# An output projection that prepares its operands two tiles ahead, with rows and values turned in squares by VectorE

## The chip, the cores and the metric

The kernel runs on one core of a Trainium2 chip. The metric is the time of one execution on the device, in microseconds (us). Before the change the median of three runs is 2102.44 us (2100.62 to 2109.52).

The engines are TensorE (PE; its weight loads are PEld), VectorE (DVE), ScalarE (ACT), GpSimd (POOL) and SyncE (SP). SP does no arithmetic here: it issues transfers, and so can ScalarE. A queue issues its transfers in order, and one that has to wait holds up those behind it.

## The reference

One inference step of a two-layer encoder, in fp32, on a prompt of 2048 tokens and on a second sequence of 32 ("sampled") tokens that carries its own state; width 1024. The kernel puts both in one list of 2080 rows, 17 tiles of 128 (the last has 32).

```
# layer 1: gated delta rule
proj = x @ w_in                      # 1024 -> 4112; short causal conv, silu, l2norm
o, s = gated_delta_rule(q, k, v, g, beta, s0)
o = rmsnorm(o) * norm_w * silu(z)    # "g" in the kernel
h = layer_norm(ALPHA * x + o @ w_out, ln_g, ln_b)
# shared keys and values of layer 2
k, v = rope(h @ w_k), h @ w_v        # 256 columns each
# layer 2: sliding-window attention with sinks
q, z = rope(h @ w_q) / 8, h @ w_z    # 1024 columns each
y = layer_norm(ALPHA * h + (attention(q, k, v) * silu(z)) @ w_out2, ln_g2, ln_b2)
```

The outputs are y for both sequences, and the new states and caches. Every large product is made of three products of fp32r operands: a value is split into a high part (a cast) and a low part (value minus high part), and high x high, high x low and low x high are summed.

## The kernel before, in words

Stages follow each other with overlaps. `P1` projects x and convolves. `Delta` runs the delta rule in chunks of 128 rows; its steps are one pipeline whose order is a string in the class (`ORDER`), with an offset for each step that says which chunk it works on. `O1` is the first layer's output projection, with its layer norm. `P2` projects h to the second layer's keys, values, queries and gates. `Attention` does the rest.

**O1.** A tile of 128 rows needs `g` (the gated outputs, columns on partitions, 128x8x128), split into `g_hi` (ScalarE) and `g_lo` (VectorE), and `r` (the rows of x). For each half of the 1024 columns (c = 0, 1) `OutNorm.tile` makes 24 matmuls into one bank of PSUM (`po`, two banks), and then VectorE adds the bank to ALPHA * r and takes statistics. After the second half VectorE makes the inverse deviation in a chain of small steps (Newton's method on one column), and normalises with two fused steps for each half (L1203, L1205), both of which read two tensors from SBUF. The rows are stored to `h`. `O1.turned` then turns them, since P2 needs columns on partitions: eight transposes on TensorE in two groups of four (L1232), into a bank each, copied by ScalarE or VectorE into `hT`, stored in pieces of 512 bytes. These two groups are issued inside the next tile's product, after its seventh and eighth step.

`O1.tiles` is a generator: it yields after every six matmuls with an estimate of their time, eight times a tile. While Delta runs, a `Filler` pulls from it: `give(0.45)` after each TensorE step of the last two rounds, and more in `first_end`. What is left runs in `second.rest()` at the end of Delta. The tile ahead is fetched at a tile's start, split after its fourth step; g has one buffer, r two, g_hi and g_lo two each.

In `rest()` TensorE and VectorE have a hand-written order (the order of the program); ScalarE, GpSimd and the queues are ordered by a planner, which may move work ahead of the place where the program has it.

`more(i)` puts other work between tiles: before tile 8 the split of P2's first operand block (`load0`), before tiles 11 to 14 a quarter each of the sums of operands that P2 needs (`presum`: four loads, four GpSimd subtractions, four stores), after tile 15 the first two products of P2 and after tile 16 the next four. `P2.go(n)` pulls n half products from `P2.stream`, which also issues weights 12 products ahead, casts them 3 ahead and makes low parts 2 ahead.

**P2.** Two pairs of 416-column blocks are multiplied with Strassen's scheme in seven products instead of eight (`group`), one block is multiplied singly. All five engines have a hand-written order here. `delay(f, n)` runs f n products later. `operand` casts an operand's four quarters on ScalarE and makes low parts on VectorE. `out_weights` is pulled one step with each product that has an operand: it loads, splits and stores the second layer's output weights, one of 16 parts every eight steps, with the cast on ScalarE two products after the load's issue. `P2.turn` turns a values product (128 columns x 416 rows): four transposes on TensorE into the bank `tp` (L1714), two copies on ScalarE, two stores from ScalarE's queue in pieces of 512 bytes. Banks of PSUM in P2: X and Z two each, Y one, tp one, two for single products.

`first_end` (in Delta) finishes the sampled chunk, which was computed first: it loads its outputs and gates, turns and gates them, stores g, and gives time to O1, all after the last chunk's step `OSC`.

## Time and profile before

| | |
|---|---|
| median of three runs | 2102.44 us (2100.62 to 2109.52) |
| profiled execution | 2110.58 us, of which the span of the profile is 2108.8 |
| TensorE, VectorE, ScalarE, GpSimd busy | 97%, 70%, 47%, 43% of the span |
| O1 alone, in its hand-written order | about 1132 to 1333 us of the span |
| P2 | about 1333 to 1740 |
| attention | 1740 to the end |

Times inside the execution are microseconds from the span's start. A row of a timeline has start, duration, engine, line, operation, and out<-in; in brackets is how long the engine stood idle before it, and what released it. A row of a group has a count, total busy time, mean in ns, and the idle time before the group's instructions. TensorE's matmuls overlap: one of 512 columns is shown with 390 ns, and the next begins 227 ns after it. The granted clock is the share of TensorE's full clock that the chip allowed in a stretch.

### The profile page before, as it was taken

What the parts mean: (1) busy time and instruction counts of PE and PEld (TensorE: products, weight loads), DVE (VectorE), ACT (ScalarE), POOL (GpSimd) and SP (SyncE); (2) the same over time, 40 slices, a digit from 0 to 9 for tenths busy, and PEclk for the clock granted to TensorE, in tenths of its full rate; (3) what the DMA queues carried; (4) which work ended last, traced back from release to release, by engine and by line L of the source; (5) the groups of instructions that cost most, each with busy time, mean ns of one, the idle gap of its engine ahead of it and who ended that gap; (6) DMA issues with size and microseconds to landing.
All of it is one profiled execution on the core that took longest, in us unless ns stands there. A gap on an engine that the chain in (4) does not pass through costs nothing.

```text
span 2108.8 us, 37301 instructions
## 1 busy us (share of the span) xinstructions
PE 2048.6 (97%) x13694; PEld 1875.4 (89%) x13694; DVE 1468.9 (70%) x2587; ACT 989.0 (47%) x2465; POOL 911.0 (43%) x1248
## 2 busy tenths in 40 slices
PE   7999999999999999999999999999999999999998
PEld 5999999999999999999887887889989997777775
DVE  4476666675647678888887887768877755566565
ACT  4354444446532267777762211534644445455552
POOL 0322223212222177778752112157436515566666
PEclk9999999999999999999999999999999999999999
DMA  5132333236665545455766666778776659533421
GB/s 206 33 90 88 97 110 111 82 102 226 193 185 179 182 137 179 159 169 182 271 209 227 212 213 219 254 229 296 243 240 222 226 171 317 127 101 107 114 72 66
DMA packets 292763, 360.85 MB, mean 171 GB/s; under 512 B 74260, under 2 KB 217460, under 8 KB 292564
## 3 DMA queue, kind: packets, MB, share of 16 engines
q1 hardware_dynamic: 278576, 334.29, 49.9%
q10 hardware_dynamic: 14004, 24.17, 3.6%
q8 instruction: 108, 1.77, 0.3%
q14 instruction: 75, 0.61, 0.1%
HBM read 235.54 MB, written 134.06 MB: 175 GB/s over the span
## 4 chain that ended last, share of the span: by engine, by line
PE 83%; DMA 7%; DVE 3%; POOL 3%; issue 2%; ACT 1%; SPq 0%; ACTq 0%; DVEq 0%; POOLq 0%
PE ps L79 12%; PE ps L81 11%; PE ps L80 11%; PE ot L1126 3%; PE ot L1127 3%; PE ot L1128 3%; PE S L1992 2%; PE po L1126 2%; PE ot L2025 2%; PE po L1128 2%; PE po L1127 2%; PE tr L2007 2%; PE X L1653 2%; PE X L1651 2%; PE X L1652 2%
## 5 line engine op out<-in xcount | busy, mean ns | idle before, releaser
L79 PE MATMUL ps<-act_hi,w_hi 128*128 128x416 f32 x1280 | 454.9, 355 | 0.0
L81 PE MATMUL ps<-act_hi,w_lo 128*128 128x416 f32 x1280 | 450.2, 352 | 0.0
L80 PE MATMUL ps<-act_lo,w_hi 128*128 128x416 f32 x1280 | 447.9, 350 | 0.0
L79 PEld LDWEIGHTS ps<-act_hi,w_hi 128*128 128x128 f32 x1280 | 240.3, 188 | 3.8 <-issue 0.4
L80 PEld LDWEIGHTS ps<-act_lo,w_hi 128*128 128x128 f32 x1280 | 240.6, 188 | 3.0
L81 PEld LDWEIGHTS ps<-act_hi,w_lo 128*128 128x128 f32 x1280 | 240.1, 188 | 3.3
L209 DVE SCALAR_TENSOR_TENSOR y<-R,convw,y 128x2083 f32<-128x2083 f32 x72 | 182.5, 2536 | 60.9 <-ACT y L206 44.9
L56 POOL TENSOR_TENSOR w_lo<-w_raw,w_hi 128x1024 fp32r<-128x1024 f32 x25 | 71.4, 2858 | 330.9 <-ACT w_hi L55 303.6
L729 POOL TENSOR_TENSOR tm<-L,Tt 128x60 f32<-128x60 f32 (+19 forms) x365 | 132.5, 363 | 84.8 <-issue 39.9
L1826 POOL TENSOR_TENSOR P<-e,sm 128x384 f32<-128x384 f32 (+2 forms) x128 | 102.3, 820 | 118.0 <-DVE sm L1816 111.6
L731 POOL TENSOR_TENSOR Tt<-Tt,tm 128x60 f32<-128x60 f32 (+19 forms) x365 | 139.8, 383 | 28.6
L1812 ACT ACTIVATE e<-S,nm 128x193 f32<-128x193 f32 (+2 forms) x260 | 104.6, 415 | 97.3 <-DVE nm L1807 56.5
L1330 DVE TENSOR_TENSOR w_lo<-w_raw,w_hi 128x512 fp32r<-128x512 f32 x132 | 136.7, 1053 | 18.5 <-ACT w_hi L1342 12.7
L1126 PE MATMUL po<-wo_hi,g_hi 128*128 128x512 f32 x256 | 104.9, 410 | 8.1 <-DVE r L1134 7.9
L305 ACT COPY R<-ps 128x416 f32<-128x416 f32 (+1 forms) x144 | 60.4, 442 | 109.3 <-PE ps L81 95.8
L1482 ACT ACTIVATE o<-X 128x416 f32<-128x416 f32 x80 | 41.4, 518 | 134.7 <-PE X L1653 134.6
L1126 PE MATMUL ot<-wo,g_hi 128*128 128x512 f32 x256 | 103.6, 405 | 0.0
L1128 PE MATMUL po<-wo_hi,g_lo 128*128 128x512 f32 x256 | 101.2, 396 | 0.5 <-DVE g_lo L1169 0.5
L1127 PE MATMUL po<-wo_lo,g_hi 128*128 128x512 f32 x256 | 101.1, 395 | 0.0
L1127 PE MATMUL ot<-wo,g_hi 128*128 128x512 f32 x256 | 100.8, 394 | 0.0
L1128 PE MATMUL ot<-wo,g_lo 128*128 128x512 f32 x256 | 100.8, 394 | 0.0
L1342 ACT CAST w_hi<-w_raw 128x512 fp32r<-128x512 f32 x129 | 76.8, 616 | 21.5 <-PE ps L1652 6.7
(362 smaller groups left out, 5119.4 us busy)
## 6 DMA issues: line engine op xcount, KB each, us to landing
w_raw<-in_b_w SPq DMA_DIRECT2D x60, 512.0 KB
w_raw<-in_w_in SPq DMA_DIRECT2D x40, 512.0 KB
act_raw<-s_hT SPq DMA_DIRECT2D x64, 208.0 KB
s_rows<-o SPq DMA_DIRECT2D x50, 208.0 KB
k<-s_k SPq DMA_DIRECT2D x17, 512.0 KB
E<-s_E SPq DMA_DIRECT2D x17, 512.0 KB
s_bq<-s_rows SPq DMA_DIRECT2D x40, 208.0 KB
s_bz<-o SPq DMA_DIRECT2D x40, 208.0 KB
```

The costliest lines, as they stand in the source:

```text
L79: nc.tensor.matmul(ps, hi[:, k, :], xh[:, k, :], start=(k == 0), stop=False)
L80: nc.tensor.matmul(ps, hi[:, k, :], xl[:, k, :], start=False, stop=False)
L81: nc.tensor.matmul(ps, lo[:, k, :], xh[:, k, :], start=False, stop=(k == KC - 1))
L209: nc.vector.scalar_tensor_tensor(out=y[:], in0=R[:, j:j + W], scalar=self.convw[:, i, j:j + 1], in1=y[:], op0=ALU.mult, op1=ALU.add)
L729: P.tensor_tensor(out=tm[:n, i0 - k:, :w], in0=L[:n, i0:, j:j + 1].to_broadcast(sh), in1=Tt[:n, j:j + 1, :w].to_broadcast(sh), op=ALU.mult)
L731: P.tensor_tensor(out=Tt[:n, i0:, :w], in0=Tt[:n, i0:, :w], in1=tm[:n, i0 - k:, :w], op=ALU.subtract)
L1126: nc.tensor.matmul(ps[:n], ghi[:, k, :n], hi, start=a, stop=False)
L1127: nc.tensor.matmul(ps[:n], ghi[:, k, :n], lo, start=False, stop=False)
L1128: nc.tensor.matmul(ps[:n], glo[:, k, :n], hi, start=False, stop=z)
L1330: P.tensor_tensor(out=lo, in0=raw, in1=hi, op=ALU.subtract)
L1812: self.nc.scalar.activation(x.e[:, h, u, :x.n], x.S[:, h, u, :], AF.Exp, bias=x.nm[:, h, u:u + 1], scale=1.0, accum_out=x.sm[:, h, u:u + 1])
L1826: self.nc.gpsimd.tensor_tensor(out=x.P[:, u, :nj * 128].rearrange("r (j h k) -> r j h k", h=2, k=64), in0=x.e[:, :, u, :n].rearrange("r h ...
```

## The change

1. **O1's pipeline.** `split` becomes `cast` (ScalarE) and `low` (VectorE). Two tiles are prepared before the loop; in tile i, after the second step, the low part of tile i+1's g (cast at the end of tile i-1) is made and g of tile i+2 is fetched. The layer norm of a tile moves into the tile after it: `scaled` after its first step, a ScalarE activation for mean and deviation after its second, `affine` (two VectorE steps over 1024 columns and the store to `h`) after its fourth, before the addition of its own first half, `turned` after its fifth, the load of the next tile's rows after its seventh. All transfers of O1 are issued by SP. The second half's bank comes from P2's two single-product banks once they exist (`spare`), so four banks are used.
2. **Rows turned by VectorE.** `turned` is one VectorE transpose that turns each 32x32 square of the 128x1024 rows in place of its square; four stores, one for each 32 partitions, put the squares in place in `hT`, in pieces of 128 bytes (32 rows of one column). The tile `hT` has two buffers; during Delta it lies in the buffers of its k.
3. **Values turned by VectorE.** `P2.turn` likewise: one transpose of 128x416, four stores on SP in pieces of 128 bytes, one to four products later. The bank tp goes, and Y has two.
4. **Other work spread.** `more(i)` is taken one step after each step of a tile: P2's first twelve steps (weights) in tiles 3 to 5, `load0` two quarters at a time in tiles 6 to 9, the sums from tile 11 on with steps between the loads, each subtraction and the stores, P2's first operand loads and two products before tile 16, four products after it.
5. **Order.** `rest()` has a hand-written order on TensorE, VectorE, ScalarE and SP. Delta's sampled end is loaded at the last round's start and done after step R, not after OSC; one more call of the generator is made before. `out_weights` begins eight steps later.

The order of O1's loop, and the new functions, from the diff:

```diff
@@ OutNorm @@
+    def bank(self, c):
+        if c and self.spare:
+            return self.spare()
+        return self.pp.tile([128, 512], F32, tag="po", name="po")
+
+    def cast(self, g, n):
         ghi = self.two.tile([128, KC, 128], F32R, tag="g_hi", name="g_hi")
+        self.nc.scalar.copy(ghi[:, :, :n], g[:, :, :n])
+        return ghi
+
+    def low(self, g, ghi, n):
         glo = self.two.tile([128, KC, 128], F32R, tag="g_lo", name="g_lo")
-        nc.scalar.copy(ghi[:, :, :n], g[:, :, :n])
-        nc.vector.tensor_tensor(out=low_part(ghi, glo, n), in0=g[:, :, :n], in1=ghi[:, :, :n], op=ALU.subtract)
+        self.nc.vector.tensor_tensor(out=low_part(ghi, glo, n), in0=g[:, :, :n], in1=ghi[:, :, :n], op=ALU.subtract)
         return ghi, glo
...
+    def scaled(self, r, n, st):
...
-                V.scalar_tensor_tensor(out=r[:n, cs], in0=r[:n, cs], scalar=mv[:n, 0:1], in1=tabs[0][:n, cs],
-                                       op0=ALU.subtract, op1=ALU.mult)
-                V.scalar_tensor_tensor(out=r[:n, cs], in0=r[:n, cs], scalar=rs[:n, 0:1], in1=tabs[1][:n, cs],
-                                       op0=ALU.mult, op1=ALU.add)
-        yield r
+        nb = self.two.tile([128, 1], F32, tag="nb", name="nb")
+        V.tensor_scalar(out=nb[:n], in0=mv[:n, 0:1], scalar1=rs[:n, 0:1], scalar2=-1.0, op0=ALU.mult, op1=ALU.mult)
+        return lambda: nc.scalar.activation(r[:n], r[:n], AF.Identity, bias=nb[:n, 0:1], scale=rs[:n, 0:1])
+
+    def affine(self, r, n, st):
+        V, tabs = self.nc.vector, self.tabs
+        V.tensor_tensor(out=r[:n], in0=r[:n], in1=tabs[0][:n], op=ALU.mult)
+        V.tensor_tensor(out=r[:n], in0=r[:n], in1=tabs[1][:n], op=ALU.add)
@@ O1 @@
     def turned(self, h, c0, row, n):
...
+        hT = self.room().rearrange("p a b -> p (a b)")
+        self.nc.vector.transpose(hT[:n], h[:n])
+        rows = self.T["hT"].rearrange("h (c j) t -> j (h c) t", j=32)
+        for a in range(0, n, 32):
+            self.nc.sync.dma_start(rows[:, :, c0 + a:c0 + a + 32],
+                                   hT[a:a + 32].rearrange("j (c i) -> j c i", i=32))
 
     def tiles(self, tiles, ready, more):
...
+            beside = itertools.chain(beside, more(i))
+            if i + 1 == len(tiles):
+                yield from (out for out in beside if out)
+            for j, out in enumerate(on.tile(parts.pop(0), r, t[2])):
+                yield out
+                next(beside, None)
+                if j == 0 and last:
+                    normalise = on.scaled(*last)
+                elif j == 1:
+                    if last:
+                        normalise()
+                    for c in coming:
+                        parts.append(on.low(g, high, c[2]))
+                    coming = tiles[i + 2:i + 3]
+                    for c in coming:
+                        while not ready(c):
+                            yield 1.0
+                        g = self.fetch(*c)
+                elif j == 3 and last:
+                    self.affine(last, *tiles[i - 1])
+                elif j == 4 and last:
+                    self.turned(last[0], *tiles[i - 1])
+                if j == 6 and i + 1 < len(tiles):
+                    following = self.rows(*tiles[i + 1])
+            for c in coming:
+                high = on.cast(g, c[2])
+            last, r = (r, t[2], on.stats), following
@@ P2 @@
-        self.py = new_pool(self.tc, left, "p2_py", 1, PSUM, side="left")
+        self.py = new_pool(self.tc, left, "p2_py", 2, PSUM, side="left")
...
     def out_weights(self):
...
+        for _ in range(8):
+            yield
...
     def turn(self, c, half, b):
...
+        nc, t = self.nc, self.out()
+        nc.vector.transpose(t[:], c[:])
...
+        def store(a):
+            s = slice(32 * a, 32 * a + 32)
+            nc.sync.dma_start(rows[a], t[s].rearrange("i (b j) -> i b j", j=32))
+
+        for a in range(4):
+            self.delay(lambda a=a: store(a), 1 + a)
@@ program @@
     def more(i):
-        if i == 0:
-            p2[0].load0()
-        elif i >= 3:
-            drain(p2[0].presum(0, p2[0].raw_act, 0, (i - 3,)))
-        else:
-            yield from p2[0].go(4 * i)
+        if 3 <= i < 6:
+            for _ in range(4):
+                next(p2[0].main)
+                yield
+        elif 6 <= i < 10:
+            yield from p2[0].load0(2 * i - 12)
+        elif 11 <= i < 15:
+            yield from p2[0].presum(0, p2[0].raw_act, 2, (i - 11,), 3)
+        elif i == 16:
+            p2[0].first_loads()
+            yield from p2[0].go(4)
+        elif i == 17:
+            yield from p2[0].go(8)
...
-    with tc.manual_schedule(engines={ET.PE}):
-        with tc.manual_schedule(engines={ET.DVE}):
-            second.rest()
+    with tc.manual_schedule(engines={ET.PE, ET.DVE, ET.Activation, ET.SP}):
+        second.rest()
```

More of the change, by code (lines that the diff above doesn't have):

```diff
@@ L1021, in first_end @@
         done(c0)
-        second.give(1.5)
     def sampled(self, pool):
@@ L1213, in __init__ @@
         self.on = OutNorm(tc, es, "o1", "left", I, "a", 2, T["wo"])
-        self.bank = lambda: self.on.pp.tile([128, 512], F32, tag="po", name="tr")
-        self.steps = 0
-        self.room = lambda: self.on.one.tile([128, KC, 128], F32, tag="g", name="hT")
+        self.steps, self.room = 0, None
     def fetch(self, c0, row, n):
@@ L1239, in tiles @@
-    def tiles(self, tiles, ready, more):
-        late = iter(())
-        got = self.fetch(*tiles[0])
+        hT = self.room().rearrange("p a b -> p (a b)")
[4 more added lines that the diff above has]
+                                   hT[a:a + 32].rearrange("j (c i) -> j c i", i=32))
+    def tiles(self, tiles, ready, more):
+        on, last, parts, beside = self.on, None, [], ()
+        for t in tiles[:2]:
+            while not ready(t):
+                yield 1.0
+            g = self.fetch(*t)
+            yield 0.0
+            parts.append(on.low(g, on.cast(g, t[2]), t[2]))
+        r = self.rows(*tiles[0])
@@ L1274 @@
+            for c in coming:
+                high = on.cast(g, c[2])
+            last, r = (r, t[2], on.stats), following
+        on.scaled(*last)()
+        self.affine(last, *tiles[-1])
+        self.turned(last[0], *tiles[-1])
+        yield from more(len(tiles))
 class P2:
@@ L1359, in take_act, with presum @@
         return t
-    def presum(self, pair, load, pace, slices=range(4)):
+    def presum(self, pair, load, pace, slices=range(4), hold=0):
         c, d = self.PAIRS[pair]
@@ L2283, in side @@
             o1.append(O1(tc, left, I, O, T, G))
+            o1[0].room = lambda: delta.four.tile([128, KC, 128], F32, tag="k", name="hT", bufs=Delta.BUFS)[:]
         else:
```

118 lines of the change are left out of this document (41 added, 77 removed).

## The prediction, made before the change had run

> **What bounds the kernel now.** I read the page's busy shares and its chain first, then windows around each stage, and in them TensorE's waits.
>
> ```profile
> PE 2048.6 (97%) x13694; PEld 1875.4 (89%) x13694; DVE 1468.9 (70%) x2587; ACT 989.0 (47%) x2465; POOL 911.0 (43%) x1248
> PE 83%; DMA 7%; DVE 3%; POOL 3%; issue 2%; ACT 1%; SPq 0%; ACTq 0%; DVEq 0%; POOLq 0%
> ```
>
> TensorE is busy 97% of the span and is 83% of the chain. So work taken off TensorE counts in full, unless another engine is nearly as long in that stage; and a wait of TensorE counts in full too. The windows show where both lie (columns: stretch, its length, busy time of PE, PEld, DVE, ACT, POOL, granted clock, DMA share, GB/s):
>
> ```profile
> 1158.90:1170.70 11.80, 11.80 (x59) 9.75 (x57) 9.25 (x21) 1.64 (x2) 0.00 (x0) 1.00 0.56 174
> 1144.00:1152.00 8.00, 5.12 (x18) 3.97 (x17) 5.99 (x14) 1.64 (x3) 3.81 (x3) 0.79 1.01 341
> 1267.00:1289.00 22.00, 16.98 (x73) 13.60 (x72) 17.03 (x36) 3.27 (x4) 7.20 (x7) 0.92 0.97 336
> 1364.00:1378.00 14.00, 9.61 (x31) 7.99 (x30) 9.98 (x13) 8.08 (x17) 6.55 (x4) 0.63 0.71 237
> 1396.00:1405.00 9.00, 6.04 (x28) 5.42 (x27) 3.36 (x7) 2.72 (x7) 3.78 (x3) 0.81 0.89 297
> 1539.00:1552.00 13.00, 8.22 (x31) 6.96 (x30) 11.76 (x17) 7.10 (x15) 4.85 (x3) 0.74 0.62 175
> 1345.00:1610.00 265.00, 251.43 (x1289) 242.34 (x1289) 202.31 (x255) 126.68 (x257) 143.13 (x91) 0.96 0.77 254
> ```
>
> The first row is one tile of the output projection: TensorE is full, VectorE is busy 9.25 of 11.8. The next five hold TensorE's longer waits, and the granted clock drops in each: the wait is paid a second time, as length times (1 - clock). The last row is the block-product stage: TensorE 95%, VectorE 76%.
>
> **Transposes off TensorE.** Each tile of 128 rows has two groups of four transposes:
>
> ```profile
> 1169.42 0.39 PE L1128 MATMUL po<-wo_hi,g_lo 128*128 128x512 f32 x1
> ...
> 1170.10 0.39 PE L1128 MATMUL po<-wo_hi,g_lo 128*128 128x512 f32 x1
> 1170.33 0.60 PE L1232 MATMUL ps<-ident,r 128*128 128x128 f32 x4
> ...
> 1171.23 0.40 PE L1128 MATMUL po<-wo_hi,g_lo 128*128 128x512 f32 x1
> ```
>
> From one L1128 to the next are 0.68 us, and 1.13 with a group between: 0.45 us a group. 17 tiles x 2 x 0.45 = 15.3 us. The second-layer values have ten groups, whose transposes last the same 272 ns, so 10 x 0.45 = 4.5 us:
>
> ```profile
> L1232 PE MATMUL ps<-ident,r x132: 221/272/273, 1119.9 to 1332.6; 128*128 128x128 f32 x124, 32*128 32x32 f32 x8
> L1714 PE MATMUL tp<-ident,o x40: 270/272/421, 1384.6 to 1600.2; 128*104 128x128 f32 x40
> ```
>
> **What VectorE gets for it.** Its period now, by the first product's addition in two tiles, and the rows for old and new operations:
>
> ```profile
> 1204.96 0.68 DVE L1134 SCALAR_TENSOR_TENSOR r<-r,po 128x512 f32<-128x512 f32 x1
> 1208.29 0.69 DVE L1234 COPY hT<-ps 128x512 f32<-128x512 f32 x1 [1.91 <-PE ps L1232]
> 1216.80 0.68 DVE L1134 SCALAR_TENSOR_TENSOR r<-r,po 128x512 f32<-128x512 f32 x1
> L1203 DVE SCALAR_TENSOR_TENSOR r<-r,mv,ln_g 128x512 f32<-128x512 f32 x32 | 27.1, 846 | 0.0
> L1205 DVE SCALAR_TENSOR_TENSOR r<-r,ln_y,ln_b 128x512 f32<-128x512 f32 x32 | 28.9, 903 | 1.1
> L1169 DVE TENSOR_TENSOR g_lo<-g,g_hi 128x1024 fp32r<-128x1024 f32 x16 | 19.5, 1220 | 1.9 <-ACT g_hi L1168 1.9
> L225 DVE STREAM_TRANSPOSE R<-th 128x2080 f32<-128x2080 f32 x16 | 37.5, 2341 | 37.8 <-ACT th L224 37.8
> L750 DVE STREAM_TRANSPOSE tcp<-tcp 128x256 f32<-128x256 f32 x16 | 7.0, 439 | 0.0
> L1881 ACT ACTIVATE r<-r,nb,ln_y 128x1024 f32<-128x1024 f32 x15 | 18.7, 1246 | 4.5 <-DVE nb L1877 4.5
> ```
>
> 11.84 us, 1.91 of it idle: 9.93 used. Out go one copy (0.69) and four fused steps (about 3.2; 3.5 by the means). In come two 128x1024 multiplications and additions at L1169's 1.22 (2.44), one small column (0.3), and a turn of 128x1024. Between L750 and L225 a turn costs 1.04 ns an element, so 0.44 + 768 x 1.04 ns = 1.24 us. That makes 10.0 to 10.4 us, against TensorE's new 11.84 - 0.90 = 10.94: VectorE stays under it, but by only 0.5 to 0.9. ScalarE's new 1.25 us runs while VectorE makes the low part (1.22); without that cover it is 1.25 us a tile on VectorE. ScalarE itself was busy 1.64 of 11.8.
>
> Two-input VectorE steps stretch beside GpSimd, where the sums run:
>
> ```profile
> 1131.52 8.44 POOL L1330 TENSOR_TENSOR w_lo<-w_raw,w_hi 128x512 fp32r<-128x512 f32 x6 [41.52 <-PE po L1127]
> 1138.73 1.78 DVE L1203 SCALAR_TENSOR_TENSOR r<-r,mv,ln_g 128x512 f32<-128x512 f32 x1
> ```
>
> 1.78 instead of the 0.85 mean, with the first row's subtractions (1.4 us each) beside it. A sum slice has four subtractions and takes nine of a generator's steps, of which a tile makes eight: some 5 us of GpSimd against 3.7 us of two-input work a tile; by chance half of it meets, +2 us in each of the five tiles 11 to 15. Bounds: 0 (the steps fall apart) to 10 us.
>
> **The rows' loop.** Rows have two buffers, as before: a tile's rows are stored, then reloaded for the tile two later. SP now also carries four stores of squares a tile, in program order ahead of that load, which is queued behind them:
>
> ```profile
> 1203.94 0.32 SPq L1265 DMA_DIRECT2D s_h<-r  x1
> 1208.28 0.33 SPq L1161 DMA_DIRECT2D r<-in_x  x1
> 1270.86 6.85 DMA s_h<-r
> 1277.78 5.76 DMA r<-in_x
> DMA packets 1046, 0.14 MB, mean 139 GB/s; under 512 B 1041, under 2 KB 1046, under 8 KB 1046
> q1 hardware_dynamic: 1046, 0.14, 88.6%
> ```
>
> Quiet, the store frees its buffer 4.3 us after issue; in the sums' stretch 6.9, and the load takes 5.8. The loop from store to usable rows is thus at most 4.3 + 5.8 = 10.1 us, or 12.6 loaded. In the new order the rows are needed one period after the store, 10.94.  The last two rows are a window of 1 us with the store of the last tile's 1024 pieces of 128 B: 0.886 x 16 / 1046 = 13.6 ns a piece, 0.9 us a store, so four take 3.5 us. They are issued 2.6 us after the rows' store (two steps on the first half, the turn), and rows behind them come after 2.6 + 3.5 + 4.3 = 10.4, the load taken like the store. Seven issues a tile at 0.32 to 0.37 leave SP free. Quiet tiles hold by 0.5; loaded ones miss by 12.6 - 10.9 = 1.7, and five make 8.5.
>
> Both effects lie in tiles 11 to 15: together 0 to 18.5 us. Low parts are made in the middle of the tile ahead of their use, which forgives VectorE half a period, some 5 us, once. I take 5. P2's first weights and block in tiles 3 to 9 I cost at nothing: GpSimd stands at 0.00 there and DMA at 0.56; were they late, the first P2 product would wait for them, as at 1364.
>
> **Waits.** The five of TensorE in the stages touched:
>
> ```profile
> PE po L1126 <- DVE r L1134: 7.9, 3, 3.8
> PE tp L1714 <- ACT o L1718: 3.0, 1, 3.0
> PE X L1651 <- ACT o L1482: 2.0, 1, 2.0
> PE Z L1651 <- DVE o L1487: 1.5, 1, 1.5
> PE X L1653 <- DVE w_lo L1330: 0.9, 1, 0.9
> ```
>
> The first line is the output projection: around 1144 VectorE stood behind a late g and the late sampled gate, around 1267 and 1280 behind rows queued after sums. Fetching two tiles ahead and the sampled end moved up take the first, spread sums the others. 7.9, and clock 8 x 0.21 + 22 x 0.08 = 3.4: 11.3 us. What is late next is the loop above, already charged.
>
> The last three lines are the first t4 product at 1364. Its cause is a ScalarE cast of output weights that waits for its transfer ahead of t4's second half:
>
> ```profile
> 1358.46 0.97 ACT L1412 CAST t4h<-act_raw 128x416 fp32r<-128x416 f32 x2
> 1363.78 0.62 ACT L1640 CAST wo_parts<-wo_parts 128x512 fp32r<-128x512 f32 x1 [4.35 <-DMA wo_parts<-in_b_w_out]
> ```
>
> Eight empty steps at the head of the output weights move that part to where the second now is. 2.0 + 1.5 + 0.9 + 14 x 0.37 = 9.6 us. The wait for tp goes with its bank and copies: 3.0 + 9 x 0.19 = 4.7 us. GpSimd, VectorE and ScalarE keep the rest of that order.
>
> Turning values adds ten 128x416 turns at 0.44 + 160 x 1.04 ns = 0.61, 6.1 us, to a VectorE that is 76% busy: 0 to 6.1, I take the uncovered quarter, 1.5. Forty stores move from ScalarE's queue to SP's, in four times the pieces, held one to four products back; an SP blocked behind one holds up weights and operands. From nothing to one wait like tp's (4.7): I take 2.5. The second bank for Y costs nothing: tp's bank pays for it.
>
> **Sum.** -15.3 - 4.5 - 11.3 - 9.6 - 4.7 + 5 + 1.5 + 2.5 = -36.4. The profiled execution took 2110.6 (span 2108.8), 8 above the median 2102.4; its waits may be a little longer than the median's, but the transposes are in all. 2110.6 - 36.4 = 2074 profiled, 2066 in the median.
>
> **Rivals.**
> *The second stage's waits only move.* For it: the row 1539-1552 shows the second pair's t4 waiting as well, with no cast of weights ahead of it, and DMA share is 0.77 in that stage. Against: the first t4's releaser is named. Without 9.6 + 4.7: 2080.
> *VectorE sets the projection's pace.* For: 10.4 against 10.94, and GpSimd beside it. Against: the stretch is long in five tiles only. At 11.84 a tile as now, 15.3 is lost and the 5 is in it: 2102.4 - 36.4 + 15.3 - 5 = 2076.
> *The spreading doesn't spread:* SP in program order blocks on sums, g or rows, and 11.3 + 14.3 us of waits return elsewhere, while the turns are won: -19.8 + 4 = 2087.
> *Slower: the store of squares paces the projection.* The 13.6 ns are of one store that left from 128 partitions; the new ones leave from 32 each, four in a row. If that doubles a piece to 27 ns, four stores take 7.0 us, and the rows come 2.6 + 7.0 + 4.3 to 5.8 = 13.9 to 15.4 us after the store: about 14.7 a tile in all 14 tiles outside Delta. The whole turns slower from 11.84 + (11.3 + 4.5 + 14.3 - 4) / 14 = 13.7 us a tile. At 14.7: 14 x 2.86 - 26.1 = +14, 2116. Against it: the row, and a DMA share of 0.56 in a tile now.
>
> The Trainium skill, "DMA: Bandwidth & Descriptors", Specifications, speaks for this last rival: below 512 B a transfer falls from line rate to read-modify-write. If each stored piece is also read, as I understand that rule, the time would be the rival's 2116; by the trace's 13.6 ns it is 2066. In that row a 128 B piece shows no such doubling.
>
> **Chances.** Forecast 0.52; waits move 0.16; VectorE 0.13; no spreading 0.11, of which 0.04 ends above 2092; slower 0.06; nothing of note 0.02. A measurement of this kernel can tell about 0.5%, 10.5 us, from no change. So faster 0.88, within 0.06, slower 0.06. Range: at the best, no new cost (-9) and the wait at 1539 gone too (13 - 8.22 + 13 x 0.26 = 8.2): 2049. At the worst the third rival with 5 us more: 2092.
>
> **What would show it.** Period of the projection's L1128 groups: 10.9 us with TensorE full confirms the transposes; above 11.5 with VectorE full is the second rival; idle VectorE before L1134 waiting for rows, the last. No TensorE wait and clock 1.00 around the 8th to 13th tile and the first t4 confirms the spreading. Per-piece time near 27 ns in those stores, or a projection stage longer than now, makes the forecast wrong.

## The result, and the profile after

| kernel | median, us | runs | ratio to before, 95% interval |
|---|---|---|---|
| before | 2103.3 | 2100.6 to 2109.5 (4) | |
| changed | 2083.0 | 2081.3 to 2085.4 (4) | 0.9900, 0.9876 to 0.9924 |

The change is faster by 20 us, 1.0%. The forecast was 36 us, 2066: the direction held and the time lies in the range given, but little more than half of the expected gain came. The profiled execution of the changed kernel took 2085.4 (span 2083.6), that of before 2110.6 (2108.8), so the two traces differ by 25.2 us, and the question is what became of the other 11.

The page of the changed kernel, its first part and the shares of its chain:

```profile
PE 2025.9 (97%) x13518; PEld 1856.4 (89%) x13518; DVE 1481.4 (71%) x2580; ACT 993.3 (48%) x2445; POOL 917.7 (44%) x1248
PE 79%; DMA 8%; DVE 6%; issue 2%; POOL 2%; ACT 1%; SPq 1%; DVEq 0%; ACTq 0%; POOLq 0%
```

TensorE has 22.7 us less to do, 2048.6 to 2025.9, and its share is still 97%. To see where in the program the time went, three marks are read in both traces: the 201st of 272 products of Delta's outputs, ahead of the stages that the change rewrites, the first block product, and the first product of the gates. First before, from the timeline and from the rows of two tiles (their last columns are the first and the last start):

```profile
1030.22 1.06 PE L876 MATMUL op<-vs,at 128*128 128x128 f32 x8
...
L1651 PE MATMUL X<-b11h,w_hi x80: 349/351/355, 1351.0 to 1701.8; 128*128 128x416 f32 x80
...
L1651 PE MATMUL ot<-act_hi,w_hi x56: 344/352/456, 1725.0 to 1770.6; 128*128 128x416 f32 x56
```

The same rows of the changed kernel:

```profile
1025.91 1.06 PE L876 MATMUL op<-vs,at 128*128 128x128 f32 x8
...
L1682 PE MATMUL X<-b11h,w_hi x80: 349/352/358, 1331.6 to 1673.5; 128*128 128x416 f32 x80
...
L1682 PE MATMUL ot<-act_hi,w_hi x56: 348/353/548, 1696.8 to 1745.2; 128*128 128x416 f32 x56
```

| stretch | before | changed | difference | forecast |
|---|---|---|---|---|
| start to the mark in Delta | 1030.2 | 1025.9 | -4.3 | 0 |
| to the first block product (projection) | 320.8 | 305.7 | -15.1 | -21.6 |
| to the first gate product (block products) | 374.0 | 365.1 | -8.9 | -14.8 |
| to the end of the span | 383.8 | 386.8 | +3.0 | 0 |

The first row can't be told from chance: in the eleven kernels below that equal the changed one up to that mark it lies anywhere from 1023.7 to 1030.7, in the one that equals the kernel before at 1029.1. Nor is the last row shown to be a loss, for it is 381.7 to 387.3 in them. The two rows between have a spread too: the projection is 305.0 to 310.0 in the three kernels below that equal the changed one there, the block products 363.8 to 367.9 in seven. What the change did is -15.1 and -8.9, 24 us in these traces, about 20 in the medians; each of the two stages fell some 6 us short.

The changed kernel's windows, columns as in the prediction: two tiles of the projection, the second at the place of the old stop at 1267; then the stretch behind the last tile; the first t4 product; and the block products.

```profile
1223.28:1234.16 10.88, 10.88 (x50) 9.01 (x49) 10.17 (x22) 2.30 (x2) 0.00 (x0) 1.00 0.85 218
1255.92:1266.80 10.88, 10.88 (x50) 9.01 (x49) 8.29 (x19) 1.05 (x1) 1.08 (x1) 1.00 0.96 313
1296.93:1314.45 17.52, 11.25 (x31) 9.10 (x31) 13.57 (x23) 7.49 (x13) 6.22 (x3) 0.61 0.50 120
1344.00:1356.00 12.00, 8.93 (x33) 7.84 (x32) 9.55 (x13) 5.05 (x11) 4.71 (x3) 0.72 0.86 294
1331.00:1580.00 249.00, 236.59 (x1211) 228.77 (x1210) 200.82 (x257) 115.79 (x229) 141.02 (x90) 0.98 0.79 257
```

TensorE's side of the projection is what it was meant to be: 10.88 us a tile, TensorE full, clock 1.00, also where it stopped before. The third row is new. Behind the last tile, the one of 32 rows, TensorE stands twice and the clock falls to 0.61. The fourth row is the old wait at t4, smaller but there. TensorE's own rows at the new stop, and ScalarE's:

```profile
1296.93 0.34 PE L1684 MATMUL ps<-act_hi,w_lo 128*128 128x416 f32 x1
1302.21 0.72 PE L1682 MATMUL ps<-act_hi,w_hi 128*128 128x416 f32 x1 [4.93 <-ACT g_lo L1144]
...
1308.08 0.71 PE L1682 MATMUL ps<-act_hi,w_hi 128*128 128x416 f32 x1 [1.34 <-ACT w_hi L1367]
```

```profile
1297.83 0.58 ACT L1144 COPY g_lo<-po 32x512 f32<-32x512 f32 x1
1301.58 0.58 ACT L1144 COPY g_lo<-ps 32x512 f32<-32x512 f32 x1 [3.18 <-DVE r L1141]
1306.28 1.24 ACT L1215 ACTIVATE r<-r,nb,ln_y 32x1024 f32<-32x1024 f32 x1 [4.12 <-DVE nb L1214]
1307.42 1.12 ACT L1367 CAST w_hi<-w_raw 128x512 fp32r<-128x512 f32 x2
```

A small tile is a short rest for TensorE but not for the others: VectorE still has the whole tile ahead of it to finish, and ScalarE copies both halves of the small one. The second half now stands in a bank of the second layer (`spare`), so the third product behind the tile waits for the copy at 1301.58; the one after waits for weights whose cast stands behind the last tile's scaling, new on ScalarE, which waits 4.12 us for VectorE. Steps of 5.3 and 1.9 us without a matmul between, and half clock from 1300.8 to 1314.4: 12.6 us in all, counted as each step between two matmuls less its full-clock length, with half a microsecond at 1288, where TensorE first waits for VectorE.

VectorE came late to this place. Its additions of a tile's first half, in the last four full tiles and the small one:

```profile
1245.83 0.69 DVE L1141 SCALAR_TENSOR_TENSOR r<-r,po 128x512 f32<-128x512 f32 x1 [0.22 <-DMA r<-in_x]
1260.23 0.69 DVE L1141 SCALAR_TENSOR_TENSOR r<-r,po 128x512 f32<-128x512 f32 x1 [2.10 <-DMA r<-in_x]
1273.63 0.69 DVE L1141 SCALAR_TENSOR_TENSOR r<-r,po 128x512 f32<-128x512 f32 x1 [1.54 <-DMA r<-in_x]
1285.69 0.67 DVE L1141 SCALAR_TENSOR_TENSOR r<-r,po 128x512 f32<-128x512 f32 x1
1296.04 0.67 DVE L1141 SCALAR_TENSOR_TENSOR r<-r,po 32x512 f32<-32x512 f32 x1
```

In the quiet tiles VectorE takes 10.4 us from one of them to the next (1214.42 to 1224.80 to 1235.16). Here three tiles take 14.40, 13.40 and 12.06, together 7.2 more than TensorE's three times 10.88. GpSimd works beside them, at the sums and then at low parts of weights, and SP carries the sums' transfers: VectorE waits for rows, as the brackets show, and steps of 1.23 us take up to 2.20. The products that these additions read ended at 1242.24, 1253.12, 1264.00 and 1274.88, so VectorE falls from 3.6 to 10.8 us behind TensorE. In the kernel before, it was 9.4 us behind in the same stretch (1274.28 to 1283.64), and TensorE, with two banks, stood. With four it runs on, and the lateness comes due behind the last tile. Had VectorE kept the distance that it had at 1245.83, these rows put the addition of the small tile's second half near 1294, before the third product needs its bank at 1297. That is an estimate from the rows of this trace, for no kernel was run without the lateness. One was run with more: in the kernel with the rotation on VectorE, below, equal up to here, VectorE adds the last full tile's second half 9.35 us after its product instead of 7.83, TensorE stands 1.85 us at 1289 besides, and the stage is 310.0.

### The profile page after: what moved, and what is told of

Its sections match the earlier page's. It is cut to its first block, busy times and chain, and to the rows that moved or that the text cites. A ratio compares the mean times of both kernels' runs of the same rounds, so it can differ in the third digit from the quotient of the medians.

```text
span 2083.6 us, 36939 instructions
## 1 busy us (share of the span) xinstructions
PE 2025.9 (97%) x13518; PEld 1856.4 (89%) x13518; DVE 1481.4 (71%) x2580; ACT 993.3 (48%) x2445; POOL 917.7 (44%) x1248
## 4 chain that ended last, share of the span: by engine, by line
PE 79%; DMA 8%; DVE 6%; issue 2%; POOL 2%; ACT 1%; SPq 1%; DVEq 0%; ACTq 0%; POOLq 0%
PE ps L79 12%; PE ps L81 12%; PE ps L80 11%; PE ot L1133 3%; PE ot L1134 3%; PE ot L1135 3%; PE S L2026 2%; PE ot L2059 2%; PE tr L2041 2%; PE X L1684 2%; PE X L1682 2%; PE X L1683 2%; PE g L695 1%; DMA w_raw<-in_b_w 1%; PE ks L846 1%
## 5 line engine op out<-in xcount | busy, mean ns | idle before, releaser
L215 DVE SCALAR_TENSOR_TENSOR y<-th,y 128x2083 f32<-128x2083 f32 x24 | 55.8, 2327 | 36.5 <-ACT th L213 36.5
L1841 DVE TENSOR_REDUCE nm<-S 128x4 f32<-128x772 f32 (+3 forms) x66 | 60.5, 917 | 15.2 <-PE S L2026 15.2
L213 ACT ACTIVATE th<-y 128x2083 f32<-128x2083 f32 x24 | 46.7, 1947 | 47.0 <-DVE y L209 43.7
```

## Experiments on the new stop

Three kernels each take one link, or both, from the changed one. The kernel before ran again beside every group of experiments, with medians of 2104.5 to 2105.4 for the 2103.3 above, so two kernels are compared by their ratios to it. The intervals are 0.3 to 0.5% wide, so a difference of two kernels is known to some 6 us, and the traces decide about less. Line numbers of the experiments differ by up to three.

**Own banks for the small tile.**

```diff
-    def bank(self, c):
-        if c and self.spare:
+    def bank(self, c, n):
+        if c and self.spare and n > 64:
```

> The changed kernel (2083.0) has a new stretch of TensorE idle behind the 32-row tile: 5.3 us from 1296.9, 1.9 from 1306.2, and a granted clock of half from 1300.8 to 1314.4, together some 13 us. This kernel gives both halves of that tile banks of their own, so that no product of the second layer waits for the second half's bank. Theory 'two links': the casts of the next weights stand on ScalarE behind the last tile's scaling (1306.3), which does not move, so the third product starts at 1297 but the fourth waits from 1299 to 1308: gain 0 to 2 us, 2081 to 2083. Rival 'the bank is the whole cause': the idle time and the half clock go, gain 11 to 13 us, 2070 to 2072.

Measured 2080.7, ratio 0.9888 (0.9867 to 0.9908). The product behind the stop in its trace:

```profile
1311.95 0.71 PE L1682 MATMUL ps<-act_hi,w_hi 128*128 128x416 f32 x1 [8.55 <-ACT w_hi L1367]
```

The third product runs at once, and the fourth waits 8.9 us for the cast instead of 5.3 and 1.9: the wait for the bank hid the one for the cast. From the mark to the first block product it is 304.7 for 305.7, no difference by the spread above. That is the theory of two links.

**The last tile's scaling behind the next products.**

```diff
+        yield from more(len(tiles))
         on.scaled(*last)()
         self.affine(last, *tiles[-1])
         self.turned(last[0], *tiles[-1])
-        yield from more(len(tiles))
```

> The changed kernel with only the order turned round: the last tile's scaling, gain and bias and turn are issued behind the next four second-layer products (their casts first), the bank of the 32-row tile is still shared. Theory 'two links': the wait for the bank stays (5.3 us from 1296.9), the one at 1306.2 goes and half clock is shorter by 1 to 3 us: gain 2 to 5, 2078 to 2081. Rival 'the bank is the whole cause': no change, 2083. Rival 'the casts are the whole cause': gain 11 to 13, 2070 to 2072.

Measured 2082.5, 0.9890 (0.9867 to 0.9912). The wait of 5.28 us for the bank is there, the second is gone, and half clock lasts 6.8 us instead of 13.7. The stage is 304.5: a new wait of 2.2 us came at 1318, and one of 2.3 at 1336, already in the block products.

**Both.**

> Both edits: own banks for the 32-row tile, and the last tile's scaling behind the next products. Theory 'two links': no TensorE idle over 1 us and clock 1.00 from 1290 to 1320, gain 11 to 13 us, 2070 to 2072. Rival 'the stall only moves on': the products that are saved here are missing later, before the first product of t4, whose operands come at the pace of the transfers; gain under 5 us, 2078 or more.

Measured 2079.2, 0.9876 (0.9855 to 0.9897); the stage is 299.6, so 6.1 us shorter than in the changed kernel and 5.4 below the shortest that equals it there; the block products, 367.9, are at the end of their spread. One long wait is left:

```profile
PE ps L1682 <- ACT w_hi L1367: 3.2, 1, 3.2
```

That cast now stands behind ScalarE's copy of the second half, which waits for VectorE at 1301.6. Both theories have a part: the links are what was said, and half of the 12.6 came back.

**The tile ahead of it later, too.** With both edits, the gain, bias and turn of the tile before the small one go behind the next products.

```diff
-                elif j == 3 and last:
+                elif j == 3 and last and t[2] > 64:
                     self.affine(last, *tiles[i - 1])
-                elif j == 4 and last:
+                elif j == 4 and last and t[2] > 64:
                     self.turned(last[0], *tiles[i - 1])
...
         yield from more(len(tiles))
+        self.affine(prev, *tiles[-2])
+        self.turned(prev[0], *tiles[-2])
```

> Own banks for the 32-row tile and the last scaling behind the next products (2079.2 so far, with 3.6 us of TensorE idle left at 1299 behind the casts), and now also the gain, bias and turn of the tile ahead of it moved behind those products, so that VectorE adds the 32-row tile's two halves 3.9 us sooner. Theory 'one chain through VectorE and ScalarE': the copies of that tile end by 1298.5 and the casts follow, idle under 1 us, no half clock there: 3 to 5 us less than without it, 2074 to 2076. Rival 'the stall only moves on': second-layer operands set the pace, no gain, 2078 to 2080.

Measured 2082.3, 0.9880 (0.9861 to 0.9899), no gain; the stage is 305.2. At 1299 TensorE now waits only 1.9 us, and at 1311 this:

```profile
PE ps L1686 <- DVE w_lo L1357: 5.6, 1, 5.6
```

The work that was pushed back on VectorE stands in front of the next low parts. The stop moves along the queue of VectorE and doesn't end, as it would if VectorE's lateness is what lies behind it; the "both" kernel is the best of these, but its interval overlaps that of the changed kernel, so nothing here is shown to beat it.

## Experiments on the projection

**The sums in one piece.**

```diff
-            yield from p2[0].presum(0, p2[0].raw_act, 2, (i - 11,), 3)
+            drain(p2[0].presum(0, p2[0].raw_act, 0, (i - 11,)))
+            yield
```

> The changed kernel with each of the four slices of the first pair's sums issued in one piece in tiles 11 to 14 (subtractions and stores without steps between them), as before the change. Theory 'the spread sums took away the stops at the 12th and 13th tile': SP's queue again holds rows and g behind stores that wait for GpSimd; TensorE waits 3 to 5 us in these tiles and pays half clock: 2087 to 2093. Rival 'fetching two tiles ahead took them away': tiles stay at 10.88 us, within 2 us of 2083.

Measured 2100.6, 0.9980 (0.9966 to 0.9994): some 17 us slower than the changed kernel, where the first theory allowed 4 to 10. The stage is 322.0 for 305.7. Its longest wait, and SP's and ScalarE's timelines around it:

```profile
PE po L1133 <- ACT g_hi L1180: 9.4, 2, 5.4
```

```profile
1254.96 3.81 SPq L1404 DMA_DIRECT2D s_sums<-act_raw  x4
1258.86 0.38 SPq L1163 DMA_DIRECT2D g<-s_g  x1
```

```profile
1263.29 1.04 ACT L1180 CAST g_hi<-g 128x1024 fp32r<-128x1024 f32 x1 [15.21 <-DMA g<-s_g]
```

The load of g stands on SP behind four stores of sums, which wait for GpSimd; g lands at 1263.3, and TensorE, whose last product began at 1258.6, stands 5.8 us. VectorE falls up to 16.9 us behind. So it is the steps between the sums that keep TensorE's tiles at 10.88, and fetching two tiles ahead doesn't make up for them. The change without them, with SP's order now written by hand, wins some 4 us.

**Each turn twice.** One more VectorE turn of 1.22 us a tile, to the same place.

```diff
-        self.nc.vector.transpose(hT[:n], h[:n])
+        for _ in range(2):
+            self.nc.vector.transpose(hT[:n], h[:n])
```

> The changed kernel (2083.0) with every turn of a projection tile's rows done twice on VectorE (17 more of 1.22 us). VectorE was busy 10.3 of 11 us in the quiet tiles, 10.2 of a 10.88 period. Theory 'VectorE stays under TensorE by 0.5 to 0.9 us': with 1.22 us more it needs 11.4 a tile and sets the pace, 0.5 us a tile less what the low parts' lead forgives: periods of 11.2 to 11.5, 4 to 9 us slower, 2087 to 2092. Rival 'its busy time hides waits of its own that shrink': period stays 10.88, within 2 us of 2083.

Measured 2101.4, 0.9974 (0.9961 to 0.9988): some 16 us slower by the ratios, not 4 to 9. A quiet tile of it, from one addition of VectorE to the next:

```profile
1220.89:1232.53 11.64, 11.20 (x50) 8.91 (x49) 10.94 (x23) 3.38 (x4) 2.14 (x2) 1.00 0.80 202
```

VectorE waits 0.18 us for ScalarE here and not for rows, and takes 11.64 where it takes 10.36 to 10.38 in the changed kernel; TensorE's tiles take the same 11.6. So VectorE sets the pace, as the first theory had it, at a period little above its 11.2 to 11.5. Its price holds too as far as the quiet tiles go: the first half of the fourteenth tile ends 234.7 us after the mark in Delta, for 227.2 in the changed kernel, 7.5 more. The other 9 us come behind that, where the sums run. VectorE is 9.5 us behind when it gets there, where it was 3.6, so what it loses to the sums now stops TensorE at once (3.15 us at 1276). This is what the four banks hid in the changed kernel.

The loop of the rows isn't far behind. In the changed kernel it reads, on SP and then on VectorE:

```profile
1203.78 0.32 SPq L1237 DMA_DIRECT2D s_h<-r  x1
1206.34 2.80 SPq L1246 DMA_DIRECT2D s_hT<-hT  x4
1209.24 0.81 SPq L1168 DMA_DIRECT2D r<-in_x  x1
```

```profile
1214.42 0.69 DVE L1141 SCALAR_TENSOR_TENSOR r<-r,po 128x512 f32<-128x512 f32 x1 [0.21 <-DMA r<-in_x]
```

From the store to the use of the new rows are 10.64 us, with VectorE waiting the last 0.21, against a period of 10.88: 0.24 us of room. The second turn lies in this loop as well, between the store and the load: there the store at 1184.93 is followed by the load at 1192.15 and the use at 1197.60, 12.67, with VectorE waiting 0.22. In the quiet tiles after that it waits for no rows.

**Each store of squares twice.** The second copy goes to an array that nothing reads.

```diff
-        rows = self.T["hT"].rearrange("h (c j) t -> j (h c) t", j=32)
-        for a in range(0, n, 32):
+        for a, d in [(a, d) for a in range(0, n, 32) for d in ("hT", "hT2")]:
+            rows = self.T[d].rearrange("h (c j) t -> j (h c) t", j=32)
```

> The changed kernel with the turned rows also stored a second time, to a second scratch array that nothing reads (four more stores of 1024 pieces of 128 B a tile). Theory of the prediction 'rows are queued behind the pieces': 3.5 us more between a tile's store and its rows' load, 13.9 against the period of 10.88: some 3 us a tile, 2120 to 2130, VectorE waiting for rows. Theory 'the transfer engines are full': their share in a tile rose from 0.56 to 0.85 to 1.0; a second set adds 0.32 and brings it over 1.0 to 1.2: 1 to 2.5 us a tile, 2098 to 2120, with g as late as the rows. Rival 'there is room': within 3 us of 2083.

Measured 2147.1, 1.0187 (1.0164 to 1.0209): some 60 us slower, and slower than before. A tile, and VectorE in it:

```profile
1178.96:1194.60 15.64, 13.10 (x50) 9.99 (x48) 10.58 (x21) 3.44 (x5) 5.28 (x3) 0.89 0.99 236
```

```profile
1173.95 0.69 DVE L1141 SCALAR_TENSOR_TENSOR r<-r,po 128x512 f32<-128x512 f32 x1 [5.08 <-DMA r<-in_x]
```

15.6 us a tile, 4.7 more than 10.88, with VectorE waiting 5.1 us for rows: the rows are queued behind the pieces, as the first theory had it, with about 1.6 times its price. SP needs 7.6 us to issue the eight stores of a tile, for 2.80 with four, so the pieces and their issue were doubled together, and this run doesn't part them. The transfer engines are full as well in this kernel (0.99), so the second theory isn't excluded as a part of it. The price of a piece in the changed kernel comes from a window of 3.8 us with hardly anything but these stores, 1227.6 to 1231.4:

```profile
DMA packets 3551, 0.46 MB, mean 120 GB/s; under 512 B 3549, under 2 KB 3549, under 8 KB 3551
q1 hardware_dynamic: 3551, 0.46, 81.0%
```

0.81 x 3.8 x 16 / 3551 = 13.9 ns a piece of 128 B, 3.6 us for a tile's 4096.

## Experiments on the block products

**Without the empty steps, and the empty steps alone.** The eight empty steps ahead of the output weights are taken out of the changed kernel, and put into the kernel before with nothing else.

```diff
-        for _ in range(8):
-            yield
         for k in range(KC):
```

> The changed kernel without the eight empty steps at the head of the output weights. The prediction's step: the cast of output weights then waits for its transfer on ScalarE ahead of t4's second half, as before the change, and the first t4 product waits 9.6 us with its half clock instead of some 7: 3 to 10 us slower, 2086 to 2093. Rival 'VectorE and GpSimd set that wait': in the changed kernel t4's low parts take 4.32 us for two (0.58 us each where GpSimd is idle) beside GpSimd's sums of weights, which the empty steps do not touch: within 2 us of 2083, and the low parts still stretched.

> The kernel before (2103 to 2105) with only the eight empty steps at the head of the output weights. The prediction's step: the cast that waits for its transfer no longer stands ahead of t4's second half, 9.6 us with the half clock, 2094 to 2095. Rival 'VectorE and GpSimd set that wait too': the cast's wait is gone, but t4's low parts meet GpSimd's sums of weights, 1.5 to 2.2 us each instead of 0.58, and TensorE still waits 3 to 4 us there with half a clock of 3.4 us: gain 2 to 5, 2099 to 2102.

Without them: 2086.2, 0.9914 (0.9893 to 0.9936), 3 us slower, which the intervals don't part from nothing; its block products are 368.5 for 365.1, just above the spread. The old cause is back on ScalarE, ahead of t4's second half, and in TensorE's waits:

```profile
1345.42 0.62 ACT L1669 CAST wo_parts<-wo_parts 128x512 fp32r<-128x512 f32 x1 [6.34 <-DMA wo_parts<-in_b_w_out]
```

```profile
PE X L1680 <- ACT o L1510: 5.5, 2, 4.7
```

The kernel before with them: 2101.2, ratio 0.9984 (0.9967 to 1.0000), 3 us and not 9.6. There ScalarE's wait is gone, but TensorE's wait for tp, further on, grows from 3.0 to 5.1, and this stands at t4 on VectorE:

```profile
1357.76 4.33 DVE L1330 TENSOR_TENSOR t4l<-act_raw,t4h 128x416 fp32r<-128x416 f32 x2
```

The changed kernel shows the same, on VectorE and on GpSimd:

```profile
1342.22 4.32 DVE L1355 TENSOR_TENSOR t4l<-act_raw,t4h 128x416 fp32r<-128x416 f32 x2
```

```profile
1343.22 1.28 POOL L1489 TENSOR_TENSOR s<-w_raw 128x512 f32<-128x512 f32 x1
1344.58 1.52 POOL L1490 TENSOR_TENSOR s<-s,w_raw 128x512 f32<-128x512 f32 x1
```

Two low parts take 4.32 us where b22's take 0.57 each, while GpSimd adds weights. TensorE makes steps of 2.25 and 1.72 us there, and the clock is at half for 6.8 us from 1348.6, which costs 3.4. So the rival holds: the named cause was real, and behind it stood a second one of nearly its size. The Trainium skill, "SBUF — State Buffer", section "SBUF: two separate sides", says that VectorE, in an instruction with two inputs from SBUF, and a GpSimd instruction that reads SBUF take one pair of ports by a lock for a whole instruction, and the other waits. The rows above agree in kind: one part grows from 0.57 to 2.16 us, by about one GpSimd instruction of 1.3 to 1.5 us.

**The rotation's product on VectorE.**

```diff
-            nc.gpsimd.tensor_tensor(out=s[:n], in0=s[:n], in1=cs[:n, 1, :], op=ALU.mult)
+            V.tensor_tensor(out=s[:n], in0=s[:n], in1=cs[:n, 1, :], op=ALU.mult)
```

> The changed kernel with the rotation's product with the sines (15 of them, 1.5 to 2.1 us each on GpSimd) done by VectorE (0.58 each where GpSimd is idle). Theory 'what is left of the t4 waits is VectorE's low parts stretched beside GpSimd': 25 us less on GpSimd, less overlap, t4's low parts under 1.7 us, TensorE's waits at the two first t4 products (2.3 and 1.6, 2.8 and 1.6 us, half clock behind each) shrink by half: gain 2 to 6, 2077 to 2081. Rival 'GpSimd's sums just start sooner and meet other low parts': VectorE has 9 us more to do at 85% busy, 2083 to 2087.

Measured 2086.0, 0.9909 (0.9892 to 0.9927). The first t4's low parts are back at 0.57, and GpSimd's sums, two microseconds sooner, meet t3's instead:

```profile
1341.57 3.07 DVE L1355 TENSOR_TENSOR t3l<-act_raw,t3h 128x416 fp32r<-128x416 f32 x2
```

and in the second pair TensorE waits 5.0 us in one place where it waited 2.8 and 1.6. The block products take 365.2 for 365.1: the collisions move and cost the same. (Its projection is 310.0, of which this edit is no cause: the first rotation comes after it.)

**Without GpSimd's sums of weights.**

```diff
-            P.tensor_tensor(out=u.s["s1"][:], in0=r2[:, a], in1=r2[:, b], op=ALU.add)
-            P.tensor_tensor(out=u.s["s2"][:], in0=u.s["s1"][:], in1=r1[:, a], op=ALU.subtract)
+            u.s["s1"], u.s["s2"] = r2[:, a], r1[:, a]
```

and likewise for the two sums that follow.

> The changed kernel without GpSimd's sums of second-layer weights (80 of them, some 130 us of GpSimd): the products take parts of the raw weights in their place, so the block products are left unsummed. Theory 'VectorE's low parts stretched beside those sums are what is left of the t4 waits': low parts back at 0.58 to 0.68 us, TensorE's 14 us of idle and 6.5 us of half clock from 1332 to 1580 mostly gone, 10 to 18 us faster, 2065 to 2073. Rival 'the transfers of operands set those waits': under 4 us faster, 2079 or more, with the waits at the same products.

Measured 2079.6, 0.9870 (0.9851 to 0.9889). The block products take 358.8, 6.3 us less, and TensorE's long steps and half clock in 1332 to 1580, counted as above, fall from 20.5 to 14.2, so the sums are about three tenths of it. My theory had nearly all. Not all of the 6.3 need be collisions: without the sums, ScalarE's casts of weights also no longer wait for GpSimd, 19 us in that stretch of the changed kernel. What TensorE still waits for, and ScalarE ahead of it:

```profile
PE ps L1681 <- DVE w_lo L1355: 3.4, 3, 2.4
PE X L1681 <- DVE w_lo L1355: 2.8, 1, 2.8
PE Z L1679 <- DVE o L1512: 2.7, 2, 2.5
```

```profile
1348.69 0.54 ACT L1440 CAST b22h<-act_raw 128x416 fp32r<-128x416 f32 x1 [2.79 <-DMA act_raw<-s_hT]
```

The stop at 1349 has moved from t4's product to b22's, whose parts wait for their transfer on ScalarE: a third cause, one product further on. How much of the 14.2 belongs to transfers and how much to the order on ScalarE was not measured.

**Values turned by TensorE, as before.** The method `turn` of P2 and the one bank for Y as in the kernel before; all else as changed.

> The changed kernel (2083.0) with the second-layer values turned by TensorE as before, with the one bank, the ScalarE copies and stores of that way; all else as changed. The prediction's terms for this part: 4.5 for ten groups of transposes and 4.7 for the wait for the bank, less 1.5 on VectorE and 2.5 on SP: 5 us slower, 2088; TensorE waits 3 us behind a transposition once. Rival 'the wait was the old order's, not the part's': 4.5 less 4, so 2082 to 2084, and no wait at a transposition over 1 us. Rival 'turns on VectorE cost nothing': 9 us slower, 2092.

Measured 2086.9, 0.9912 (0.9894 to 0.9930): 2.5 us slower by the ratios, 3.9 by the medians; block products 368.8 for 365.1, 0.9 above the longest of their spread. One transposition waits:

```profile
1376.63 1.09 PE L1745 MATMUL tp<-ident,o 128*104 128x128 f32 x4 [4.07 <-ACT o L1749]
```

The wait for tp belongs to the part and not to the old order. The forecast's 5 is within what the runs can tell, and so is nothing at all; the trace alone speaks for a gain.

## Why the prediction was half right, step by step

| step of the sum | forecast | what the runs show |
|---|---|---|
| rows' transposes off TensorE | -15.3 | -16.3: 11.84 to 10.88 a quiet tile, times 17 as in the forecast |
| values' transposes, tp's wait, less VectorE and SP | -5.2 | -2.5 by the ratios, not clear of chance |
| projection's stops | -11.3 | gone where they were |
| rows' loop, sums beside VectorE | +5 | 7.2 on VectorE, none on TensorE there; 12.6 on TensorE behind the small tile |
| first t4 product | -9.6 | about -3: two more causes stood behind the first |

The projection's rows come to -16.3 - 11.3 + 12.6 = -15.0, for the -15.1 between the marks. That 2083 lies in the range is in part luck: its upper end was drawn for a spreading that fails with SP blocked, and what used it up was a stop behind the last tile and a wait that stayed.

- *Transposes.* Right: period 10.9 with TensorE full was the mark named for it.
- *VectorE.* Right in size: 10.0 to 10.4 forecast, 10.36 to 10.38 from addition to addition in quiet tiles, and a turn of 1.23 us (17 of them, 20.8 us) for 1.24:

```profile
L1243 DVE STREAM_TRANSPOSE hT<-r 128x1024 f32<-128x1024 f32 (+1 forms) x17 | 20.8, 1226 | 0.0
```

- *Rows' loop.* Quiet, 10.4 forecast and 10.64 measured, against 10.88: by the forecast it holds, and it did. Loaded, 12.6 forecast, and 12.82 from the store at 1247.41 to the use at 1260.23. One reading was wrong: "seven issues a tile at 0.32 to 0.37 leave SP free". The four stores of squares take SP 2.80 us in a quiet tile and more beside the sums:

```profile
1248.42 6.23 SPq L1246 DMA_DIRECT2D s_hT<-hT  x4
```

- *The term of 5.* Here the first step fails: "What is late next is the loop above, already charged." The loop and the sums did make VectorE late, by 7.2 us where 5 were charged. But the prediction took that for a time that TensorE would wait in those tiles. It left out that four banks let TensorE run on, and that the lateness then falls due all at once, with the half clock behind it: 12.6. I had gone through the loop of the full tiles and not to its end. The change does two things there that I read in the diff and never followed: the 32-row tile's second half goes to a bank of P2, and the scaling that is new on ScalarE stands ahead of the weights' casts, with manual order now on ScalarE too. The prediction had "ScalarE's new 1.25 us runs while VectorE makes the low part": true in the quiet tiles (VectorE waits 0.18 us) and not for the last two scalings, which have no such low part to cover them (1.31 us each). That the lateness is what made these two links bind is worked out above and was not run.
- *The sign for the spreading.* "No TensorE wait and clock 1.00 around the 8th to 13th tile" came true, and TensorE doesn't stop up to the 16th tile. But VectorE is later then (10.8 us in the 16th) than it was before the change (9.4 in the 14th), so the two more banks have a part in it that the sign can't tell. The kernel with the sums in one piece shows the spreading's own part.
- *First t4 product.* The second step that fails: "9.6 us" taken whole from one named releaser. A releaser is the one that came last; taking it away gives the distance to the one before, here about 3 us (0 to 7 by the interval). The first rival said this ("the second stage's waits only move", 2080, 0.16) and is nearest to what happened, though with another mechanism than the one quoted for it.
- *The other rivals.* VectorE doesn't set the pace of the quiet tiles, by half a microsecond; in the loaded ones it is slower than TensorE, for the three tiles that the banks can hide. The spreading does spread, and is worth some 17 us in SP's new order. The slower rival's mechanism is real: with the pieces' time doubled I had 13.9 to 15.4 us a tile by the loop, and the doubled stores gave 15.6. Its price was wrong: a piece takes 13.9 ns, not 27, by the row of a single store 13.6. The Trainium skill, "DMA: Bandwidth & Descriptors", Specifications, has transfers under 512 B turn to read-modify-write; no doubled price is seen in these pieces. They are half the price of a 512 B piece, 27 ns in the trace of before (the 1024 of the store issued at 1209.04).
- *The base.* The sum was made against an execution 7 us above the median. Of the traces' 25.2 us, 20.3 are in the medians, and I had taken 36 from both.

## What to carry to other kernels

Take a wait's length as its worth only after looking for the one that stands second: in this kernel, taking the last releaser away gave 3 us of 9.6, and one link of two gave no more than 1 of 12.6. Where tiles are made faster, follow the order of every engine past the last, odd tile as well, for it gives TensorE less to do and the other engines the same. A bottleneck engine that never stops is no sign that the engine behind it keeps up: measure how far behind it each tile is, for more buffers turn that engine's loss into a debt, paid where the buffers run out. A margin measured with one more unit of the suspected cost (a turn, a store) shows this debt, as the doubled turn did.

## What the runs showed of the hardware

- The granted clock fell to half in stretches that are multiples of 3.41 us (3.4, 6.8, 10.2, 13.7 in these traces, the last stretch of each span apart), and after idle times shorter than one of them: 1.85 us at 1289 in the kernel with the rotation on VectorE (2.25 from start to start) was followed by 3.41 us at half, and 1.90 us at 1346 in the changed kernel by 6.8. The Trainium skill, "TensorE: Matmul & The Clock Gate", section "What's actually happening", has a window of 3.413 us, which agrees; its idle time of at least a whole window for the fall doesn't agree with those stops.
- Stores of 1024 pieces of 128 B from 32 partitions cost the same per piece, 13.9 ns, as one from 128 partitions, 13.6.
- Kernels that are equal up to the mark in Delta reach it at 1023.7 to 1030.7 us. Two profiles alone would have shown 4 us of that as an effect of the change. Part of it is the clock: with no half-clock stretch ahead of the mark it is reached at 1023.7 to 1025.9 (five traces, the changed kernel's among them), with one of 3.41 us at 1025.3 to 1027.7 (six), with two at 1029.1, with three at 1030.2 (the kernel before) and 1030.7.
